# One substitution per group of heads, and both directions' B and Q from one operation, in a hybrid RWKV-7 and attention layer

## The chip, the cores and the metric

The kernel runs on 1 core of a Trainium2 chip. The metric is the device time of one execution in microseconds (us). Before the change it was 1323.57 us, the median of 3 runs (1322.31 to 1329.43).

## What is computed

One layer over 256 latent tokens that read 256 context tokens, width 2048, all in fp32. After a modulated norm, one wide projection feeds two branches: a bidirectional RWKV-7 recurrence with 16 heads of 64, and a latent attention with 8 heads. Both are gated, merged and projected out. The change concerns the recurrence. For each head and direction:

```python
def rwkv7_step(S, xs):
    r, w, k, v, kk, akk = xs
    sa = jnp.einsum("dbhij,dbhj->dbhi", S, -kk)
    S = S * w[..., None, :] + sa[..., :, None] * akk[..., None, :] + v[..., :, None] * k[..., None, :]
    return S, jnp.einsum("dbhij,dbhj->dbhi", S, r)
```

Here kk is the key made a unit vector per head, akk is a * kk with a = sigmoid(...), w is the decay, and k is k * (1 + (a - 1) * k_a). The scan runs over the context and from its last state over the latent tokens, forwards and backwards.

## The kernel before

**Stages.** The modulation and the first projections come first (to about 150 us), then the RWKV stage, to about 900 us, then the attention, then the merge and the output. Projections that nobody waits for soon ("background", tile acc on PE) are strung between the small matmuls of the heads. Each 256 KB piece of weights (tile w, four buffers) is loaded by SP and split into a high and a low part, wh by ACT and wl by DVE; every product is three matmuls (helper mm3).

**The chunked recurrence.** A pair p of heads is one tile of 128 partitions, 64 for each. In the code h counts pairs twice: an even h is the context half of pair h // 2, an odd one its latent half. A half has 4 chunks of 64 tokens in 2 directions, so 8 units, each for two heads. In each unit the step is a lower (or upper) triangular system of 64x64. `front` builds it. It makes th (tanh for a), the sums of the log decay and their exponentials Ep and En, the modified keys km, Q from kk and Ep (in Qbd for a context half, in QR for a latent one), and B and K beside each other in BK. Matmuls of BK with Q give the system, and DVE masks it into AQ.

**The inverse.** `diagonal` inverts the 16x16 blocks on the diagonal of these systems. Eight DMAs write a half's 64 blocks from AQ to DRAM (dl); one DMA reads them back with one block a partition (ln); two copies turn the second direction's blocks round; 14 pairs of DVE operations (pr, then wt) substitute; ACT makes a turned copy; one DMA writes both to DRAM (dw); and eight DMAs put them into WT, the block-diagonal inverse (WTs[0] for context halves, WTs[1] for latent ones). The chain is called a lane. Before, each half has its own lane, appended to `lanes` inside `front`, and the lanes run one after the other. A lane ends only when the levels of the group before are done, since they read WT.

**Groups.** `back` takes a group: halves 2k-1 and 2k, the latent half of one pair and the context half of the next; the first and the last group hold one half, the seven others two. It first builds the whole inverse from WT in levels (matmuls into lv, results in W2 and Z), then goes through the four chunks (tile chp). It starts when both halves' lanes are done (`inverted > hs_[-1]`).

**The order.** `drive` lines the generators up: `back_chain`, `front_chain`, the queue of finals and the queue of lanes, with background work where none may go on. Its clock adds a price for each instruction, so another count of DVE instructions gives another order. A scheduler then sorts each engine's instructions by priority (the lane's substitution runs under `tc.high_priority(HS)`) and by its own estimate of readiness. Every engine and SP's queue work strictly in the order that results. The background list holds gate projections (narrow: 256 columns), keys and values (wide: 512 columns) and others; what the heads' stage leaves is run to the query projections before the attention begins.

Of the kernel before, what the change touches and what calls it, by code (L numbers as in the profile page):

```python
# [9 lines left out]
F32 = mybir.dt.float32  # L10
# [6 lines left out]
P = 128  # L17
# [109 lines left out]
def hybrid_block(  # L127
# [442 lines left out]
    with tc.tile_pool(name="rw", bufs=1) as rw:  # L570
# [99 lines left out]
        def front(h, k, mi, rho):  # L670

            p, lat = h // 2, h % 2
            if not lat:
# [1 line left out]
            ck = cks[p]  # L675
            kk, cr = kks[p], crs.get(p)
            t0 = 0 if lat else T
            WT = WTs[lat]
# [59 lines left out]
            ex = [slice(0, 64), slice(1, 65)]  # L738
            kkc = kk[:, ts].rearrange("p (c t) -> p c t", t=CH)
            for d in range(2):  # L740
                if lat:
                    V.scalar_tensor_tensor(Q[:, d, :, 0], kkc, -1.0, Ep3[d][:, :, ex[d]], ALU.mult, ALU.mult)
                else:
                    for g in range(2):
                        hs = hss[g]
                        V.scalar_tensor_tensor(Q[hs, d, :, g], kkc[hs], -1.0, Ep3[d][hs, :, ex[d]], ALU.mult, ALU.mult)
            BK = rw.tile([P, 8, 2, CH], F32, name="BK", bufs=2)
            BK5 = BK.rearrange("p (d c) a t -> p d c a t", d=2)
            for g in range(2):
                hs = hss[g]  # L750
                for d in range(2):
                    V.scalar_tensor_tensor(BK5[hs, d, :, g], v4(th)[hs, d], 0.5, En3[d][hs, :, ex[1 - d]], ALU.mult, ALU.mult)
                V.tensor_tensor(BK5[hs, :, :, 1 - g], v4(km)[hs], ecols(En, 1, 0)[hs], ALU.mult)
            if lat:
                V.tensor_tensor(Q[:, :, :, 1], dirs(cr), ecols(Ep, 1, 0), ALU.mult)
# [89 lines left out]
                yield  # L845
            halves[h] = (Q, AQ, AR, BKT)

        def diagonal(group, AQ, WT):

            dl = dram.tile([8, 8, 16, 16], F32, name="dl", tag="dl")  # L850
            for g in range(2):
                for b in range(4):
                    r0 = 64 * g + 16 * b
                    nc.sync.dma_start(dl[:, 4 * g + b].rearrange("u r c -> r u c"), AQ[r0:r0 + 16, g, :, 16 * b:16 * b + 16])
            yield LT[0]
            ln = rw.tile([64, 16, 16], F32, name="ln", tag="ln")
            nc.sync.dma_start(ln.rearrange("p r c -> p (r c)"), dl.rearrange("u h r c -> (u h) (r c)"))
            yield LT[1]
            with tc.high_priority(HS):
                wt = rw.tile([64, 2, 16, 16], F32, name="wt")  # L860
# [3 lines left out]
                pr = rw.tile([64, 16, 16], F32, name="pr", tag="ln")  # L864
                for k in range(14, 0, -1):

                    m = 15 - k
                    V.tensor_tensor(pr[:, 0:k, 0:m], X[:, 0:k, k:k + 1].to_broadcast([64, k, m]),
                                    X[:, k, k + 1:16].unsqueeze(1).to_broadcast([64, k, m]), ALU.mult)
# [3 lines left out]
            dw = dram.tile([2, 8, 8, 16, 16], F32, name="dw", tag="dw")  # L873
            yield LT[2]
            nc.sync.dma_start(dw.rearrange("w u h r c -> (u h) w (r c)"), wt.rearrange("p w r c -> p w (r c)"))
            yield LT[3]
            yield lambda: levels >= group
            WTu = WT.rearrange("p w u t -> p (w u) t")
            for g in range(2):
                for b in range(4):  # L880
                    r0 = 64 * g + 16 * b
                    nc.sync.dma_start(WTu[r0:r0 + 16, :, 16 * b:16 * b + 16],
                                      dw[:, :, 4 * g + b].rearrange("w u r c -> r (w u) c"))
            yield LT[4]
            nonlocal inverted
            inverted += 1
# [209 lines left out]
        def front_chain():  # L1096
            nonlocal keyed, fronts
            for k, hs_ in enumerate(groups):
                rho = rw.tile([P, 2, 10], F32, name="rho", bufs=3)
                for m, h in enumerate(hs_):  # L1100
                    p = h // 2
                    yield (lambda: p in cks and (h % 2 == 0 or p in crs))
                    yield from front(h, k, m, rho)
# [466 lines left out]
```

## Time and profile before

| what | value |
|---|---|
| runs | 1323.57 us median, 1322.31 to 1329.43 |
| profiled execution | 1325.01 us, its span 1323.2 us |
| mean granted clock | 0.988 |
| PE, DVE, ACT busy | 95%, 72%, 43% of the span |
| chain that ended last | PE 63%, DMA 17%, DVE 13%, ACT 3% |
| DMA | 212.10 MB, 160 GB/s on average |

PE is TensorE's matmuls, PEld its weight loads, DVE is VectorE, ACT is ScalarE, POOL is GpSimd, SP the queue that issues the DMAs. L103 and L122 are lines of helpers that all matmuls and all elementwise operations pass, so instructions are told apart by their tiles: "wt<-wt,pr" writes wt from wt and pr. A line of groups gives the count, then the busy time and the mean duration in ns, then the engine's idle time before and what ended it. PE's ends are modelled and overlap, so its rate is read from the starts of successive matmuls.

### The profile page before, as it was taken

Reading aid. Unit: us, or ns where it says so; the run is one execution under the profiler, and the core shown is the slowest. Engines: PE = TensorE matmul, PEld = TensorE weight load, DVE = VectorE, ACT = ScalarE, POOL = GpSimd, SP = SyncE. Lnnn points to the kernel's source line nnn. Section 1 sums busy time; section 2 is a strip of 40 time slices with the busy share of each in tenths; the row PEclk is TensorE's granted clock in tenths of the full one; section 3 lists DMA queues with packets and bytes.
Section 4 is the critical chain, followed back from the end, with each engine's and each line's share of the span. In section 5 each row is a group of like instructions: output and inputs, shape, how many; then the busy total and the mean of one; then the engine's idle time right before and its main releaser. Section 6 shows DMA issues by size and latency. Waiting matters only on the chain.

```text
span 1323.2 us, 30169 instructions
## 1 busy us (share of the span) xinstructions
PE 1255.7 (95%) x11484; PEld 1048.0 (79%) x11484; DVE 948.6 (72%) x2658; ACT 570.9 (43%) x1183; POOL 3.3 (0%) x9
## 2 busy tenths in 40 slices
PE   5999888999999999999999999999899999999998
PEld 2656777888887877787788798779788889899776
DVE  4444866878888888878888788655787775468655
ACT  3344532453433524534344245244566645345443
POOL 0000000000000000000000000000000000000000
PEclk9999987999999999999999999999999999999999
DMA  9998554453444423534344244225643326778665
GB/s 375 346 352 298 160 156 120 145 156 90 110 108 127 141 73 95 150 92 124 93 126 141 59 130 130 69 67 174 203 139 104 102 81 217 234 247 272 215 218 175
DMA packets 172320, 212.10 MB, mean 160 GB/s; under 512 B 68560, under 2 KB 96848, under 8 KB 171664
## 3 DMA queue, kind: packets, MB, share of 16 engines
q1 hardware_dynamic: 172176, 210.18, 51.7%
q8 instruction: 90, 1.47, 0.5%
q14 instruction: 54, 0.44, 0.1%
HBM read 195.30 MB, written 14.82 MB: 159 GB/s over the span
## 4 chain that ended last, share of the span: by engine, by line
PE 63%; DMA 17%; DVE 13%; ACT 3%; issue 2%; SPq 1%; DVEq 0%; ACTq 0%
PE acc L103 28%; PE chp L103 11%; PE lv L103 8%; PE wk L103 6%; DMA w<-in_w_proj 5%; DVE wl L122 4%; DMA wm<-in_w_mod_ss 4%; PE a L103 3%; PE ch L103 2%; DMA w<-in_w_out 2%; DVE BK L122 2%; PE wk L107 2%; ACT wh L122 2%; DMA th<-thd 1%; DMA xT<-in_xcT 1%
## 5 line engine op out<-in xcount | busy, mean ns | idle before, releaser
L122 ACT CAST wh<-w 128x512 fp32r<-128x512 f32 (+1 forms) x484 | 290.8, 607 | 387.6 <-PE acc L103 168.2
L122 DVE TENSOR_TENSOR wl<-w,wh 128x512 fp32r<-128x512 f32 (+1 forms) x480 | 322.3, 675 | 150.7 <-ACT wh L122 62.9
L103 PE MATMUL acc<-hmh,wh 128*128 128x256 f32 (+1 forms) x1328 | 423.6, 319 | 6.1 <-ACT wh L122 3.7
L103 PE MATMUL acc<-hml,wh 128*128 128x256 f32 (+2 forms) x1328 | 407.9, 307 | 0.0
L103 PE MATMUL acc<-hmh,wl 128*128 128x256 f32 (+1 forms) x1312 | 401.4, 306 | 3.7 <-DVE wl L122 3.3
L103 PEld LDWEIGHTS acc<-hmh,wh 128*128 128x128 f32 x1328 | 252.3, 190 | 33.2 <-ACT wh L122 7.8
L103 PEld LDWEIGHTS acc<-hmh,wl 128*128 128x128 f32 x1312 | 248.9, 190 | 20.8 <-DVE wl L122 7.9
L103 PEld LDWEIGHTS acc<-hml,wh 128*128 128x128 f32 (+1 forms) x1328 | 251.7, 190 | 10.9 <-issue 1.0
L122 DVE TENSOR_TENSOR pr<-wt 64x14 f32<-64x14 f32 (+6 forms) x224 | 42.5, 190 | 2.5
L122 DVE TENSOR_TENSOR wt<-wt,pr 64x14 f32<-64x14 f32 (+6 forms) x224 | 42.3, 189 | 2.4
L122 DVE TENSOR_TENSOR W<-WT,lv 128x512 f32<-128x512 f32 x48 | 32.7, 684 | 14.4 <-PE lv L103 9.4
L103 PE MATMUL a<-hmh,wh 128*128 128x512 f32 x96 | 41.2, 429 | 0.0
L103 PE MATMUL pm<-wm,ssil 128*32 128x256 f32 x512 | 34.7, 386 | 5.0 <-DMA wm<-in_w_mod_ss 4.9
L103 PE MATMUL a<-hmh,wl 128*128 128x512 f32 x96 | 38.7, 403 | 0.4 <-DVE wl L122 0.4
L103 PE MATMUL lv<-W,Z 64*64 64x64 f32 x1024 | 36.8, 226 | 2.3 <-issue 1.3
L103 PEld LDWEIGHTS lv<-W,Z 64*64 64x64 f32 x1024 | 33.6, 140 | 6.4 <-DVE W L122 1.9
L103 PE MATMUL a<-hml,wh 128*128 128x512 f32 x96 | 38.4, 400 | 0.0
L103 PE MATMUL chp<-obh,wl 128*128 128x256 f32 x128 | 36.5, 285 | 0.3 <-DVE wl L122 0.3
L103 PE MATMUL chp<-obh,wh 128*128 128x256 f32 x128 | 36.2, 283 | 0.0
L103 PE MATMUL chp<-obl,wh 128*128 128x256 f32 x128 | 36.2, 283 | 0.0
L122 DVE TENSOR_TENSOR AQ<-wk,cc 128x256 f32<-128x256 f32 (+1 forms) x48 | 24.4, 509 | 14.4 <-PE wk L103 12.8
L122 ACT ACTIVATE hx<-hx,mod 128x256 f32<-128x256 f32 x32 | 17.5, 594 | 37.8 <-DVE mod L122 37.8
(314 smaller groups left out, 2120.1 us busy)
## 6 DMA issues: line engine op xcount, KB each, us to landing
w<-in_w_proj SPq DMA_DIRECT2D x296, 256.0 KB, 3.0
wm<-in_w_mod_ss SPq DMA_DIRECT2D x64, 512.0 KB, 7.5
w<-in_w_mod_g SPq DMA_DIRECT2D x64, 256.0 KB, 3.4
w<-in_w_br SPq DMA_DIRECT2D x64, 256.0 KB, 3.5
w<-in_w_out SPq DMA_DIRECT2D x64, 256.0 KB, 3.3
w<-in_w_first SPq DMA_DIRECT2D x32, 192.0 KB, 5.2
thd<-th SPq DMA_DIRECT2D x48, 128.0 KB, 2.7
xT<-in_xcT SPq DMA_DIRECT2D x4, 1024.0 KB, 8.9
```

Source lines behind the costliest of these rows:

```text
L103: return self.engine.matmul(out, lhsT=lhsT, rhs=rhs, **kw)
L107: return self.engine.transpose(*a)
L122: return fn(out, *a, **kw)
```

## The change

The lane is made once for a group. `front` only sends its half's blocks out (`blocks_out`), into one of two places of a dl that the group shares. When both halves of the group are through `front`, `diagonal` is appended; it reads up to 128 blocks to 128 partitions, makes four copies, one substitution and one turned copy, writes dw in one DMA for each half, and fills both WT with eight DMAs each. `back_chain` waits for the group's one lane (`inverted > k`).

In `front` the minus sign of Q goes into rnb, the spread inverse norm, so kk is negated from there on. ACT turns th into -0.5 * th - 0.5 in place, and with the negated kk the product is what B held before with its factor 0.5. Q and B are then plain products for both directions in one operation: one for a latent half's Q in place of two, two for a context half's Q in place of four, and two for B in place of four.

```diff
-            V.tensor_copy(rnb.rearrange("p (a c) -> p a c", c=CH), rn.unsqueeze(2).to_broadcast([P, 8, CH]))
+            V.tensor_scalar(rnb.rearrange("p (a c) -> p a c", c=CH), rn.unsqueeze(2).to_broadcast([P, 8, CH]), -1.0, None, ALU.mult)
...
-            V.scalar_tensor_tensor(v4(th), v4(th), 1.0, dirs(kk[:, ts]), ALU.add, ALU.mult)
+            S.activation(th, th, AF.Copy, scale=-0.5, bias=-0.5)
+            V.tensor_tensor(v4(th), v4(th), dirs(kk[:, ts]), ALU.mult)
...
-            for d in range(2):
-                if lat:
-                    V.scalar_tensor_tensor(Q[:, d, :, 0], kkc, -1.0, Ep3[d][:, :, ex[d]], ALU.mult, ALU.mult)
-                else:
-                    for g in range(2):
-                        hs = hss[g]
-                        V.scalar_tensor_tensor(Q[hs, d, :, g], kkc[hs], -1.0, Ep3[d][hs, :, ex[d]], ALU.mult, ALU.mult)
+            kkd = dirs(kk[:, ts])
+            if lat:
+                V.tensor_tensor(Q[:, :, :, 0], kkd, ecols(Ep, 0, 1), ALU.mult)
+            else:
+                for g in range(2):
+                    hs = hss[g]
+                    V.tensor_tensor(Q[hs, :, :, g], kkd[hs], ecols(Ep, 0, 1)[hs], ALU.mult)
...
-                for d in range(2):
-                    V.scalar_tensor_tensor(BK5[hs, d, :, g], v4(th)[hs, d], 0.5, En3[d][hs, :, ex[1 - d]], ALU.mult, ALU.mult)
+                V.tensor_tensor(BK5[hs, :, :, g], v4(th)[hs], ecols(En, 1, 0)[hs], ALU.mult)
...
-            lanes.append(diagonal(k, AQ, WT))
+            blocks_out(AQ, dl[mi])
...
+        def diagonal(group, n, dl, at):
+
+            np_ = 64 * n
             yield LT[0]
-            ln = rw.tile([64, 16, 16], F32, name="ln", tag="ln")
-            nc.sync.dma_start(ln.rearrange("p r c -> p (r c)"), dl.rearrange("u h r c -> (u h) (r c)"))
+            ln = rw.tile([P, 16, 16], F32, name="ln", tag="ln")[0:np_]
+            nc.sync.dma_start(ln.rearrange("p r c -> p (r c)"), dl[0:n].rearrange("m u h r c -> (m u h) (r c)"))
...
-                V.tensor_copy(X[0:32], ln[0:32])
-                V.tensor_copy(X[32:64], ln[32:64].rearrange("p r c -> p c r"))
+                for q in range(2 * n):
+                    qs = slice(32 * q, 32 * q + 32)
+                    V.tensor_copy(X[qs], ln[qs].rearrange("p r c -> p c r") if q % 2 else ln[qs])
...
-            nc.sync.dma_start(dw.rearrange("w u h r c -> (u h) w (r c)"), wt.rearrange("p w r c -> p w (r c)"))
+            for m in range(n):
+                nc.sync.dma_start(dw[m].rearrange("w u h r c -> (u h) w (r c)"),
+                                  wt[64 * m:64 * m + 64].rearrange("p w r c -> p w (r c)"))
...
+            for m in range(n):
+                WTu = WTs[at[m]].rearrange("p w u t -> p (w u) t")
+                for g in range(2):
+                    for b in range(4):
+                        r0 = 64 * g + 16 * b
+                        nc.sync.dma_start(WTu[r0:r0 + 16, :, 16 * b:16 * b + 16],
+                                          dw[m, :, :, 4 * g + b].rearrange("w u r c -> r (w u) c"))
...
+                lanes.append(diagonal(k, len(hs_), dl, [h % 2 for h in hs_]))
...
-                yield (lambda: k in ready and inverted > hs_[-1] and sums_ >= k - 1)
+                yield (lambda: k in ready and inverted > k and sums_ >= k - 1)
```

The order moves with it. Three places in a middle group follow, each before and after. First SP, from the read of the blocks (ln) to the first blocks of the next latent half; WT_1360 is the latent halves' inverse, WT_1358 the context halves'. Before, for the context half alone:

```order
L857 DMA ln<-dl 64x256
L214 DMA w<-in_w_mod_g 128x512
L214 DMA w<-in_w_proj 128x512 x4
L451 DMA thd<-th 128x256
L214 DMA w<-in_w_proj 128x512 x4
L1053 DMA orwd<-y 128x256
L214 DMA w<-in_w_mod_g 128x512 x2
L682 DMA th<-in_wup 128x256
L875 DMA dw<-wt 64x2x256
L882 DMA WT_1358<-dw 16x16x16 x8
L214 DMA w<-in_w_proj 128x512 x3
L854 DMA dl<-AQ 16x8x16 x8
```

And now, for both halves:

```order
L857 DMA ln<-dl 128x256
L214 DMA w<-in_w_mod_g 128x512 x2
L214 DMA w<-in_w_proj 128x512 x2
L1057 DMA orwd<-y 128x256
L877 DMA dw<-wt 64x2x256 x2
L214 DMA w<-in_w_proj 128x512 x2
L886 DMA WT_1360<-dw 16x16x16 x8
L886 DMA WT_1358<-dw 16x16x16 x8
L850 DMA dl<-AQ 16x8x16 x8
```

The latent half's dw and WT moved from ahead of this place into it, and eleven loads of w between ln and dw became four.

Second PE, from the last projection ahead of the context half's first level to the levels of W. Before:

```order
L103 MATMUL acc<-hmh,wh 128x512
L103 MATMUL wk<-QR,BK 128x128 x3
L103 MATMUL lv<-WT_1358,AQ 64x64 x15
L103 MATMUL wk<-QR,BK 128x128 x4
L103 MATMUL lv<-WT_1358,Z 64x64 x16
L103 MATMUL wk<-QR,BK 128x128
L103 MATMUL lv<-W_5635,Z 64x64 x32
L103 MATMUL acc<-hml,wh 128x512
L103 MATMUL acc<-hmh,wl 128x512
L103 MATMUL wk<-QR,BK 128x128 x8
```

And now:

```order
L103 MATMUL acc<-hmh,wl 128x256
L103 MATMUL wk<-cc,sq 128x2 x4
L103 MATMUL lv<-WT_1358,AQ 64x64 x15
L103 MATMUL chp<-UV,AQ 64x64
L103 MATMUL lv<-WT_1358,Z 64x64 x16
L103 MATMUL lv<-W_5360,Z 64x64 x64
L103 MATMUL chp<-UV,AQ 64x64 x3
L103 MATMUL acc<-hmh,wh 128x256
```

The next latent half's QR matmuls went ahead of the levels, and the four rounds of W stand in one run.

Third ACT, at the start of a latent half's `front`, where th and En come from the two low-rank products in wk. Before:

```order
L122 ACTIVATE th<-acc 128x256
L122 COPY wt<-wt 64x256
L122 ACTIVATE th<-wk,dv 128x256 x2
L122 ACTIVATE En<-wk,dv 128x4x64 x2
L122 ACTIVATE En<-En 128x2x4x64
L122 CAST wah<-th 128x256
L122 CAST wh<-w 128x512
L122 COPY AQ<-QR 64x512
L122 ACTIVATE En<-Ep 128x260 x2
L122 ACTIVATE Ep<-Ep 128x260 x2
```

And now:

```order
L122 ACTIVATE th<-wk,dv 128x256 x2
L122 ACTIVATE En<-wk,dv 128x4x64 x2
L122 ACTIVATE th<-th 128x512
L122 CAST wh<-w 128x512
L122 COPY wt<-wt 128x256
L122 ACTIVATE En<-En 128x2x4x64
L122 ACTIVATE cv<-acc,vv 128x512
L122 ACTIVATE En<-Ep 128x260 x2
L122 ACTIVATE Ep<-Ep 128x260 x2
```

The new step th<-th stands between the tanh and the exponentials, and the turned copy of wt, now of 128 partitions, moved behind the tanh.

More of the change, by code (lines that the diff above doesn't have):

```diff
@@ L668, in unit_keys, with front @@
             kks[p] = kk
-        def front(h, k, mi, rho):
+        def front(h, k, mi, rho, dl):
             p, lat = h // 2, h % 2
@@ L677, in front @@
             t0 = 0 if lat else T
-            WT = WTs[lat]
             ts = slice(t0, t0 + T)
@@ L737, in front @@
             Q = rw.tile([P, 2, 4, 2, CH], F32, name="QR", bufs=2) if lat else Qbd
-            ex = [slice(0, 64), slice(1, 65)]
-            kkc = kk[:, ts].rearrange("p (c t) -> p c t", t=CH)
-            for d in range(2):
-                if lat:
-                    V.scalar_tensor_tensor(Q[:, d, :, 0], kkc, -1.0, Ep3[d][:, :, ex[d]], ALU.mult, ALU.mult)
-                else:
-                    for g in range(2):
-                        hs = hss[g]
-                        V.scalar_tensor_tensor(Q[hs, d, :, g], kkc[hs], -1.0, Ep3[d][hs, :, ex[d]], ALU.mult, ALU.mult)
+            kkd = dirs(kk[:, ts])
[5 more added lines that the diff above has]
+                    V.tensor_tensor(Q[hs, :, :, g], kkd[hs], ecols(Ep, 0, 1)[hs], ALU.mult)
             BK = rw.tile([P, 8, 2, CH], F32, name="BK", bufs=2)
@@ L846, in front2, with blocks_out @@
             halves[h] = (Q, AQ, AR, BKT)
-        def diagonal(group, AQ, WT):
-            dl = dram.tile([8, 8, 16, 16], F32, name="dl", tag="dl")
+        def blocks_out(AQ, dl):
             for g in range(2):
@@ L872, in diagonal @@
                 S.copy(wt[:, 1], X.rearrange("p r c -> p c r"))
-            dw = dram.tile([2, 8, 8, 16, 16], F32, name="dw", tag="dw")
+            dw = dram.tile([2, 2, 8, 8, 16, 16], F32, name="dw", tag="dw")
             yield LT[2]
-            nc.sync.dma_start(dw.rearrange("w u h r c -> (u h) w (r c)"), wt.rearrange("p w r c -> p w (r c)"))
+            for m in range(n):
+                nc.sync.dma_start(dw[m].rearrange("w u h r c -> (u h) w (r c)"),
+                                  wt[64 * m:64 * m + 64].rearrange("p w r c -> p w (r c)"))
             yield LT[3]
             yield lambda: levels >= group
[L878 to L883, printed above, removed]
+            for m in range(n):
[5 more added lines that the diff above has]
+                                          dw[m, :, :, 4 * g + b].rearrange("w u r c -> r (w u) c"))
             yield LT[4]
@@ L1099, in front_chain @@
                 rho = rw.tile([P, 2, 10], F32, name="rho", bufs=3)
+                dl = dram.tile([2, 8, 8, 16, 16], F32, name="dl", tag="dl")
                 for m, h in enumerate(hs_):
@@ L1102, in front_chain @@
                     yield (lambda: p in cks and (h % 2 == 0 or p in crs))
-                    yield from front(h, k, m, rho)
+                    yield from front(h, k, m, rho, dl)
                     keyed += 1
+                lanes.append(diagonal(k, len(hs_), dl, [h % 2 for h in hs_]))
                 yield lambda: backs >= k
```

8 lines of the change are left out of this document (4 added, 4 removed).

## The prediction

> **What bounds the kernel now.** I read the page first, then the sums by stage, the waits of the middle stage, the groups by shape, and the timeline of one group of heads. The page gives the span and the engines:
>
> ```profile
> span 1323.2 us, 30169 instructions
> PE 1255.7 (95%) x11484; PEld 1048.0 (79%) x11484; DVE 948.6 (72%) x2658; ACT 570.9 (43%) x1183; POOL 3.3 (0%) x9
> ```
>
> The profiled execution took 1325.0 us by its own clock, 1.8 over its span and 1.4 over the median of 1323.6. I make the sum against 1325.0 and take 1.4 off at the end. The change touches only the RWKV part, so its stages matter. The columns are the stretch, its length, busy time of PE, PEld, DVE, ACT and POOL, the granted clock, the DMA share and GB/s:
>
> ```profile
> 200.00:245.00 45.00, 40.86 (x399) 35.41 (x397) 31.05 (x104) 13.85 (x28) 0.00 (x0) 0.85 0.49 144
> ...
> 476.00:564.00 88.00, 84.14 (x941) 69.87 (x940) 71.88 (x222) 35.15 (x75) 0.00 (x0) 1.00 0.41 112
> 564.00:651.00 87.00, 84.75 (x949) 70.29 (x945) 72.67 (x223) 35.13 (x75) 0.00 (x0) 1.00 0.41 113
> ...
> 1108.00:1131.00 23.00, 23.00 (x198) 23.00 (x198) 12.24 (x19) 11.43 (x22) 0.00 (x0) 1.00 0.75 225
> ```
>
> Two middle groups of heads take 88 and 87 us each. PE is idle for 3.9 and 2.3 us of them, DVE for 16.1 and 14.3 us, ACT for more than half. So PE sets the pace of a group, and its small gaps are all that faster work elsewhere can return. The gaps that have a releaser on DVE, between 250 and 880 us (what waited, then the total, the number of waits and the longest):
>
> ```profile
> ACT wh L122 <- PE acc L103: 113.1, 55, 13.4
> ...
> PEld wk L103 <- DVE BK L122: 5.3, 5, 1.2
> PEld wk L103 <- DVE QR L122: 4.7, 4, 1.2
> ...
> PEld chp L107 <- DVE rvb L122: 4.2, 6, 0.9
> ```
>
> PE waits for DVE 14.2 us in the three largest rows (5.3 + 4.7 + 4.2); in most others the engine that waits is ACT or DVE, and it waits for PE. That is how a stage reads whose bound is PE.
>
> **The change, part by part.** The durations (busy total, mean ns of one) by shape:
>
> ```profile
> L122 DVE TENSOR_TENSOR pr<-wt 64x14 f32<-64x14 f32 (+6 forms) x224 | 42.5, 190 | 2.5
> L122 DVE TENSOR_TENSOR wt<-wt,pr 64x14 f32<-64x14 f32 (+6 forms) x224 | 42.3, 189 | 2.4
> ```
>
> ```profile
> L122 DVE SCALAR_TENSOR_TENSOR BK<-th,En 64x256 f32<-64x256 f32 x64 | 24.6, 416 | 0.5
> L122 DVE TENSOR_TENSOR BK<-km,En 64x512 f32<-64x512 f32 x32 | 21.8, 682 | 0.1
> L122 DVE SCALAR_TENSOR_TENSOR Qbd<-kk,Ep 64x256 f32<-64x256 f32 x32 | 13.3, 417 | 0.4
> L122 DVE TENSOR_TENSOR km<-km,ck 128x512 f32<-128x512 f32 x16 | 11.0, 687 | 0.2
> L122 DVE SCALAR_TENSOR_TENSOR th<-th,kk 128x512 f32<-128x512 f32 x16 | 10.8, 674 | 0.0
> ...
> L122 DVE SCALAR_TENSOR_TENSOR QR<-kk,Ep 128x256 f32<-128x256 f32 x16 | 6.0, 410 | 0.0
> L122 DVE TENSOR_TENSOR QR<-cr,Ep 128x512 f32<-128x512 f32 x8 | 5.5, 690 | 0.1
> ```
>
> ```profile
> L122 ACT COPY wt<-wt 64x256 f32<-64x256 f32 x16 | 10.2, 638 | 4.8 <-DVE wt L122 4.5
> L122 ACT ACTIVATE En<-En 128x512 f32<-128x512 f32 x16 | 10.1, 634 | 0.4
> ```
>
> 1. *One substitution a group.* There are 16 now, one a head, and 9 afterwards, one a group (seven groups of two heads, two of one). The elements a partition stay the same and only the partitions double; the 64x256 operation at 417 ns and the 128x256 one at 410 show that partitions cost nothing. So 7/16 of 42.5 + 42.3 = 84.8 us go: 37.1 us of DVE. The copies out of ln stay 32. ACT's turned copy goes from 16 to 9: 7 x 0.638 = 4.5 us less.
> 2. *B and Q of both directions from one operation.* B: 64 operations of 24.6 us become 32 like the km row, 21.8: 2.8 less. Q of context heads: 13.3 us become 16 x 0.682 = 10.9: 2.4 less. Q of latent heads: 6.0 become 8 x 0.690 = 5.5: 0.5 less. The product with kk is a plain one, 11.0 for 10.8: 0.2 more. The sign put into rnb turns a copy into an operation with a constant:
>
> ```profile
> L122 DVE TENSOR_SCALAR km<-th,dv 128x512 f32<-128x512 f32 x16 | 8.7, 541 | 5.3 <-ACT th L122 5.3
> ...
> L122 DVE COPY rnb<-rn 128x512 f32<-128x512 f32 x8 | 3.3, 415 | 0.1
> ```
>
> At most that is 8 x (0.541 - 0.415) = 1.0 us more, at least nothing; the km row has two constants, this one has one, and I take nothing.
>
> 3. *A new step on ACT.* The factor -0.5 and the shift of th become an ACT operation like the En row: 16 x 0.634 = 10.1 us. ACT as a whole: 10.1 - 4.5 = 5.6 more, at 43% busy.
>
> DVE is thus 37.1 + 2.8 + 2.4 + 0.5 - 0.2 = 42.6 us lighter. Almost all of that lies beside PE's work, which covers it. What reaches the end is the part of 14.2 us that PE waits for DVE. A group's DVE time falls from 72 to about 66 us; I let half of the waits go: 7 us, with 0 and 14 as ends.
>
> *The ACT step on the path.* B now waits for DVE, ACT and DVE again. In ACT's order the step stands between the tanh and the exponentials of the same head, which B and Q wait for anyway; so a head's B comes at most 0.63 us later. PE waited at B or Q nine times: 9 x 0.63 = 5.7 us at most, 0 at least, and I take 3, the middle, as some waits vanish with the lighter DVE. By the Trainium skill ("TensorE: Matmul & The Clock Gate", the section on the array of 32x32 blocks) ACT's queue is strictly first in, first out, so the step would stand behind any ACT instruction that waits: at the mean wait of the wh row, 113.1/55 = 2.1 us, nine times make 19 us in place of 3. The trace agrees that ACT holds its place (13.4 us at one wh); I keep 3 because nothing new stands ahead of the step.
>
> *PE's order.* The matmuls are the same in number. What differs is how often PE goes from one kind to another. Counted in the two orders, neighbours that write different tiles are 922 before and 865 after, 57 fewer, most of them between projections (acc) and the small matmuls of the heads. What one costs:
>
> ```profile
> 487.50 0.28 PE L103 MATMUL acc<-hml,wh 128*128 128x256 f32 x1
> ...
> 487.61 0.28 PE L103 MATMUL acc<-hmh,wl 128*128 128x256 f32 x1
> 487.82 0.19 PEld L103 LDWEIGHTS chp<-AR,UV 128*64 128x64 f32 x2
> 487.82 0.33 PE L103 MATMUL chp<-AR,UV 128*64 128x64 f32 x2
> ...
> 488.08 0.39 PE L103 MATMUL acc<-hmh,wh 128*128 128x256 f32 x1
> ```
>
> Projections follow each other at 0.11 us. The detour takes 487.61 to 488.08, 0.47; less 0.11 it is 0.36 for two switches and two small passes, so at most 0.18 a switch; the way out alone is 0.21 - 0.11 = 0.10. With 0.10 to 0.18, 57 are 6 to 10 us. I take 0.12, near the lower end since the passes are in the upper one: 7 us less.
>
> *Projections moved behind.* The order of a middle group holds 48 narrow projections fewer than before (144 or so for 192), and the last group begins with 42 narrow and 104 wide ones more left over. They run after the heads, where PE is dense (23.00 of 23.00 us in a stretch of such work); each costs there what it cost before. Zero, as long as weights arrive; the DMA share of 0.75 there is the cover.
>
> *One lane a group.* The blocks of a group now go out, through the substitution and back as one chain, which starts when the second head is ready. The chain of the second head before, on SP, DVE and PE:
>
> ```profile
> 523.56 3.65 SPq L854 DMA_DIRECT2D dl<-AQ  x8
> ...
> 549.02 0.63 SPq L875 DMA_DIRECT2D dw<-wt  x1
> 551.77 3.77 SPq L882 DMA_DIRECT2D WT<-dw  x8
> ```
>
> ```profile
> 534.77 0.67 DVE L122 COPY wt<-ln 32x256 f32<-32x256 f32 x2
> ...
> 548.10 0.17 DVE L122 TENSOR_TENSOR wt<-wt,pr 64x14 f32<-64x14 f32 x1
> ```
>
> ```profile
> 521.64 1.16 PE L103 MATMUL wk<-Qbd,BK 128*128 128x128 f32 x8
> ```
>
> ```profile
> 549.84 0.40 PE L103 MATMUL acc<-hml,wh 128*128 128x512 f32 x1
> 550.08 0.39 PE L103 MATMUL acc<-hmh,wl 128*128 128x512 f32 x1
> 550.40 1.15 PE L103 MATMUL lv<-WT,AQ 64*64 64x64 f32 x32
> ...
> 556.53 0.27 PE L103 MATMUL lv<-WT,AQ 64*64 64x64 f32 x1
> ```
>
> ```profile
> WT<-dw SPq DMA_DIRECT2D x128, 16.0 KB, 2.1
> ```
>
> Before, the latent head's inverse was long in place (its lane ran ahead) and only the context head's was late. Now dw is two DMAs and WT sixteen in a row. From the last Qbd matmul at 521.6: WT would begin at 551.77 + 0.63 = 552.4; the latent eight are issued by 556.2 and landed 2.1 us later, 36.7 us after that matmul; the context eight 3.8 us later, at 40.4. What covers it on PE: the first level matmul came 28.8 us after, with 27 wide and 96 narrow projections between; now there are 78 and 48. At 0.24 (550.08 less 549.84) and 0.11 that is 17.0 before and 24.0 after, 7 us more: 35.8 for the latent head, and some 41 for the context one, which came 6.1 us behind it and comes nearly as far behind now. Need and cover agree within a microsecond, so I put 0 here, with a loss as the open end. Behind WT on SP stand eight dl DMAs of the next latent head (3.65 us), and behind those the weights that ACT's wh waits for; PE has the levels to do meanwhile, which need none.
>
> Sum: -7 (waits for DVE) + 3 (ACT step) - 7 (switches) + 0 + 0 = -11: 1325.0 - 11 = 1314.0, on the scale of the median 1312.6 us.
>
> **The rivals.**
>
> *A: the lane comes late (slower).* It is one mechanism: PE, in order, stands at the first level matmul of a group until the sixteen WT DMAs have landed. The price is seven groups times the lateness. For it: the cover above has no margin, and between ln and dw SP has few weight loads, so a substitution later than planned also holds up weights that queue behind dw. Against it: DVE is lighter, and the substitution took 13.3 us (534.77 to 548.10) for some 5.3 us of its own work, so it can shorten. It decides from about 2.5 us a group: 7 x 2.5 = 17.5 brings 1312.6 to 1330. At 4 us a group, the time of the eight added WT DMAs, it is 28 us: 1341. The trace shows what idling adds: 0.85 of the clock in 200 to 245, where PE idled 4.1 of 45 us. The Trainium skill (same page, the part on the HAM clock gate) has the clock halved after an idle window of about 3.4 us and given back after a busy one; an estimate by that page is 1.7 us more for each stall of 4 us, 12 in all, and 1353. Here only the 0.85 bears on it.
>
> *B: DVE sets the pace after all (much faster).* DVE works in order at 72 of 88 us. If each of PE's starts hung on it, the whole 42.6 us would show: 1281, and with half of it 1302. Against it: PE's 2.3 to 3.9 idle us a group.
>
> *C: nothing that can be measured.* The waits stay, at other places, and the switches were covered: 1325.0 - 0 to 5, so 1318 to 1324 on the median's scale.
>
> **How the numbers follow.** My forecast has 0.48. Its own ends are 1300 (14 and 10 less, no cost of the step) and 1323 (6 less, 5.7 more), with most of the chance between 1303 and 1319. A has 0.18 (1330 to 1345), B 0.12 (1281 to 1302), C 0.22. About 0.5% (6.6 us, so 1317 to 1330) is what a measurement can tell from no change here. Faster by more: 0.43 of the forecast and all of B, 0.55. Within: 0.05 of the forecast and C, 0.27. Slower: A, 0.18. The range leaves a tenth on each side: the faster part of B below 1296, the slower half of A above 1337.
>
> **What would show it.** Right: DVE busy near 906 us and ACT near 576, 126 each of pr and wt at 190 ns, PE idle in a middle group no more than 3 us, its cycle about 80 us, and the long dense stretch after the heads some 30 us longer. The switch term: PE's busy time falls by 5 us or more. Wrong: PE rows that wait for WT<-dw or, behind it, for w, at the first lv of a group (A); PE's idle time in the groups unchanged and the span with it (C); a group's cycle at 75 us or less with the same stretch behind it (B).

## The result, and the profile after

The changed kernel takes 1338.88 us (median of 4 runs, 1337.81 to 1341.97), the kernel before 1322.94 (4 runs, 1317.63 to 1329.43). The ratio is 1.0123, 95% interval 1.0089 to 1.0156: slower by 1.2%. The prediction said 1312.6 and had its chance of 0.55 on faster; it had the wrong sign, and the time lies above its range, which ended at 1337.

The first lines of the page of the changed kernel, whose profiled execution took 1337.81 us:

```profile
span 1336.0 us, 29950 instructions
PE 1253.1 (94%) x11484; PEld 1050.9 (79%) x11484; DVE 926.1 (69%) x2399; ACT 577.5 (43%) x1192; POOL 3.3 (0%) x9
```

PE is busy 2.6 us less than before and the span is 12.8 us longer: PE stands idle 15.4 us more. To see where, here are the sums by stage. The first row of each kernel runs from the end of the first group's levels to the end of the last group's; the second goes on to the start of the attention. The kernel before:

```profile
227.00:878.00 651.00, 634.42 (x6990) 528.90 (x6989) 528.86 (x1609) 261.25 (x566) 0.00 (x0) 1.00 0.40 112
878.00:930.00 52.00, 50.56 (x485) 45.70 (x482) 30.85 (x90) 22.52 (x52) 0.00 (x0) 1.00 0.50 150
```

The changed kernel:

```profile
230.00:860.00 630.00, 595.22 (x6789) 503.15 (x6788) 496.08 (x1336) 255.84 (x549) 0.00 (x0) 0.98 0.39 108
860.00:948.00 88.00, 85.54 (x660) 73.58 (x655) 42.06 (x112) 33.35 (x75) 0.00 (x0) 0.98 0.45 137
```

The heads end earlier, because projections were moved behind them, and the stretch behind grows by more: 651 + 52 = 703 us before, 630 + 88 = 718 after. Of these 15 us, PE's idle time among the heads is 18.2 (651 - 634.4 = 16.6 before, 630 - 595.2 = 34.8 after) and that behind them 1.0; PE's busy time in both falls by only 4.2. The last column but two is TensorE's granted clock, as a share of full speed: 1.00 before, 0.98 after. Rows around the places where it falls, in the changed kernel:

```profile
545.00:552.00 7.00, 5.52 (x111) 4.87 (x112) 4.60 (x13) 1.35 (x3) 0.00 (x0) 0.76 0.57 176
702.00:715.00 13.00, 11.11 (x134) 9.83 (x134) 7.61 (x21) 1.72 (x3) 0.00 (x0) 0.61 0.29 87
736.00:743.00 7.00, 6.73 (x86) 5.63 (x86) 2.43 (x7) 2.79 (x8) 0.00 (x0) 0.76 0.08 27
794.00:804.00 10.00, 4.82 (x26) 4.60 (x27) 4.72 (x9) 4.50 (x10) 0.00 (x0) 0.66 0.47 130
```

If the clock is half there and full outside, the half-clock times are 7 x 0.24 x 2 = 3.4 us, then 10.1, 3.4 and 6.8: 23.7 us among the heads, which cost at most half of it, 11.9. They are inside PE's busy time, so without them that time would have fallen by 4 to 16 us, not by 4.2.

Waits between 250 and 880 us in the kernel before (what waited, for what, then the total, the number of waits and the longest):

```profile
PE wk L103 <- DVE QR L122: 3.0, 4, 0.8
...
PE acc L103 <- ACT wh L122: 0.5, 2, 0.2
```

and in the changed kernel:

```profile
PE wk L103 <- DVE QR L122: 7.6, 5, 3.3
...
PE acc L103 <- ACT wh L122: 6.8, 2, 6.2
```

The waits of PE at QR have become longer each (up to 3.3 us, 0.8 before), and PE waits 6.2 us for one split weight (wh).

The longest wait at QR in the timeline, whose columns are the start, the duration, the engine and what ran (in brackets the wait ahead of it and what ended it), on SP first:

```profile
695.10 7.80 SPq L886 DMA_DIRECT2D WT<-dw  x16
703.00 0.39 SPq L214 DMA_DIRECT2D w<-in_w_mod_g  x1
```

and then on PE, where the next row of projections comes only at 715:

```profile
700.28 0.33 PE L103 MATMUL lv<-WT,AQ 64*64 64x64 f32 x2
703.89 1.19 PE L103 MATMUL wk<-QR,BK 64*128 64x128 f32 x6 [3.29 <-DVE QR L122]
705.01 1.96 PE L103 MATMUL lv<-WT,AQ 64*64 64x64 f32 x30
```

For 7.8 us SP issues WT and no weights. From 700.3 us on PE has the levels, the next head's QR and no projection. It stands 3.3 us at QR, and the 30 level matmuls that follow take 1.96 us; 32 took 1.15 before, at the full clock.

Of the 6.8 us at wh, 6.2 are one wait, at 799, and it does not stand behind WT. SP ahead of it:

```profile
783.85 0.43 SPq L1419 DMA_DIRECT2D gd<-gT  x1
784.95 3.96 SPq L214 DMA_DIRECT2D w<-in_w_proj  x3
789.95 1.24 SPq L877 DMA_DIRECT2D dw<-wt  x2
...
801.58 7.70 SPq L886 DMA_DIRECT2D WT<-dw  x16
```

and the DMAs issued from 783 to 797 us, with KB each and the median time from issue to landing:

```profile
w<-in_w_proj SPq DMA_DIRECT2D x5, 256.0 KB, 12.0
dw<-wt SPq DMA_DIRECT2D x2, 128.0 KB, 11.4
```

Each kernel issues gd once: 8 KB that it writes to DRAM one element of 4 bytes at a time (of the 2532 DMA packets in that stretch 2115 are under 512 B). What SP issues around and behind it here lands after 11 to 12 us, where from 200 to 783 us the medians are 3.0 for w and 2.4 for dw. ACT's split of such a weight, PE behind it and SP's own WT wait for these. In the kernel before SP issues nothing in the 7 us behind its gd. The 25 us from gd's issue, first before, then after:

```profile
735.00:760.00 25.00, 23.45 (x356) 20.11 (x352) 17.22 (x53) 4.57 (x10) 0.00 (x0) 1.00 0.23 49
783.90:808.90 25.00, 18.48 (x161) 17.11 (x162) 16.75 (x44) 10.56 (x23) 0.00 (x0) 0.86 0.41 79
```

PE's idle time there is 1.6 us before and 6.5 after, and the clock costs at most 25 x 0.14 = 3.5 us more. So by an estimate from these rows up to 8 us of the loss lie where the new order has put other DMAs behind gd. No run moved gd, so this is read from the traces and not shown by an experiment.

### The profile page after: what moved, and what is told of

The parts are those of the page before. It is cut to its first block, busy times and chain, and to the rows that moved or that the text cites. A ratio compares the mean times of both kernels' runs of the same rounds, so it can differ in the third digit from the quotient of the medians.

```text
span 1336.0 us, 29950 instructions
## 1 busy us (share of the span) xinstructions
PE 1253.1 (94%) x11484; PEld 1050.9 (79%) x11484; DVE 926.1 (69%) x2399; ACT 577.5 (43%) x1192; POOL 3.3 (0%) x9
## 4 chain that ended last, share of the span: by engine, by line
PE 37%; DMA 9%; DVE 7%; ACT 2%; issue 1%; SPq 1%; DVEq 0%; ACTq 0%
PE acc L103 16%; PE chp L103 8%; PE lv L103 6%; PE wk L103 3%; PE ch L103 3%; DVE wl L122 2%; DMA w<-in_w_proj 2%; DMA th<-thd 1%; DMA w<-in_w_out 1%; PE wk L107 1%; DMA thd<-th 1%; DMA dw<-wt 1%; ACT wh L122 1%; DVE wt L122 1%; DMA ln<-dl 1%
## 5 line engine op out<-in xcount | busy, mean ns | idle before, releaser
L122 ACT CAST wh<-w 128x512 fp32r<-128x512 f32 (+2 forms) x484 | 291.2, 607 | 378.6 <-PE acc L103 134.4
L103 PE MATMUL acc<-hml,wh 128*128 128x256 f32 (+1 forms) x1328 | 405.3, 305 | 0.0
L103 PEld LDWEIGHTS acc<-hmh,wl 128*128 128x128 f32 x1312 | 248.8, 190 | 23.7 <-DVE wl L122 10.6
L103 PEld LDWEIGHTS acc<-hml,wh 128*128 128x128 f32 x1328 | 251.4, 189 | 11.1 <-issue 0.9
L103 PE MATMUL pm<-wm,ssil 128*32 128x256 f32 x512 | 34.8, 385 | 5.6 <-DMA wm<-in_w_mod_ss 5.4
L103 PE MATMUL wk<-QR,BK 64*128 64x128 f32 x256 | 25.3, 308 | 10.7 <-DVE QR L122 7.6
L103 PE MATMUL chp<-UV,AQ 128*64 128x64 f32 x512 | 30.2, 235 | 3.7 <-ACT AQ L122 2.4
L103 PEld LDWEIGHTS pm<-wm,ssil 128*32 128x32 f32 x512 | 13.3, 109 | 24.6 <-DMA wm<-in_w_mod_ss 13.3
```

The source lines that it names most:

```text
L103: return self.engine.matmul(out, lhsT=lhsT, rhs=rhs, **kw)
L122: return fn(out, *a, **kw)
```

## The experiments

Each run is given as the ratio to the kernel before on the same chip. Four theories stood at the start. Theory 1, lost cover: the planner's clock is charged less for DVE, so a group holds fewer projections, and PE stands among the small matmuls. Theory 2, the merged lane. Theory 3, the ACT step and the merged B and Q make QR late. Theory 4: any other order moves the time by a per cent.

**One half of the change at a time.** The first run has only the B and Q half:

```diff
-            V.scalar_tensor_tensor(v4(th), v4(th), 1.0, dirs(kk[:, ts]), ALU.add, ALU.mult)
+            S.activation(th, th, AF.Copy, scale=-0.5, bias=-0.5)
+            V.tensor_tensor(v4(th), v4(th), dirs(kk[:, ts]), ALU.mult)
...
-                for d in range(2):
-                    V.scalar_tensor_tensor(BK5[hs, d, :, g], v4(th)[hs, d], 0.5, En3[d][hs, :, ex[1 - d]], ALU.mult, ALU.mult)
+                V.tensor_tensor(BK5[hs, :, :, g], v4(th)[hs], ecols(En, 1, 0)[hs], ALU.mult)
```

with Q and the sign in rnb likewise.

> The kernel before with the B and Q half of the change alone (sign in rnb, ACT step on th, merged Q and B); the lanes are as before, one a half. In its order the middle groups still hold 208 narrow and 96 to 99 wide projections, and 1392 narrow ones stand behind the heads, as before. Theory 1 (the loss is cover: the order puts fewer projections among the small matmuls of a group, and PE stands there for DVE and ACT): no change from before, 1316 to 1328. Theory 2 (the merged lane: its longer chain on SP and DVE is late, or holds up the weights behind it): no change or a few us less, 1312 to 1326. Theory 3 (the ACT step and the merged operations make B and Q late): the loss is here, 1333 to 1342. Theory 4 (any other order moves the time by about 1% either way): anything from 1310 to 1340.

Measured: 1314.55 us for 1316.53, ratio 0.9978 (0.9958 to 0.9998). The waits of PE at BK and QR between 250 and 880 us did not grow:

```profile
PEld wk L103 <- DVE QR L122: 3.3, 3, 1.3
PEld wk L103 <- DVE BK L122: 3.3, 4, 1.0
```

They are 4.7 and 5.3 us before, and PE's idle time among the heads is 13.2 us for 16.6. Theory 3 falls: this half is no loss, if anything a small gain.

The second run has only the lane:

```diff
-            lanes.append(diagonal(k, AQ, WT))
+            blocks_out(AQ, dl[mi])
...
+                lanes.append(diagonal(k, len(hs_), dl, [h % 2 for h in hs_]))
```

> The kernel after with the B and Q half taken back: only the merged lane is new. The order is close to that of after: the middle groups hold 124 to 221 narrow projections, and 1488 stand behind the heads (1434 in after, 1392 before). Theory 1 (lost cover): slow like after or a little worse, 1333 to 1345. Theory 2 (the lane itself): the same, 1333 to 1345. Theory 3 (ACT step, late B and Q): back at the level of before, 1316 to 1328.

Measured: 1357.87 us, ratio 1.0303 (1.0276 to 1.0331). The loss is in the lane and the plan that comes with it, and larger than in the whole change.

**Cover, and a control for the plan.** LF is the part of a chain's planned latency that the planner waits before its next step.

```diff
-LF = 0.6
+LF = 0.75
```

> The kernel after with one number of the planner changed: LF 0.75 for 0.6, so that each step of a chain waits a larger part of the planned latency and more projections are put between. All instructions are those of after, in another order: the middle groups hold 193 to 208 narrow and 96 wide projections, 1392 stand behind the heads, as before. Theory 1 (lost cover): the loss goes, 1305 to 1325, and PE's idle time among the heads falls from 46 us to the 23 us of before. Theory 2 (the lane itself): the loss stays, 1332 to 1345, with PE or the split of the weights waiting behind dw and WT. Theory 3: stays too, 1332 to 1345, with waits for QR and BK.

Measured: 1342.79 us, ratio 1.0204 (1.0171 to 1.0237). The groups are as full as before and the loss is not smaller. Theory 1 in this form falls. PE's idle time among the heads is 25.0 us in place of 34.8.

The same number at 0.62 in the kernel before:

> The kernel before with the planner's LF at 0.62 for 0.6: the same instructions in a slightly other order (1362 narrow projections behind the heads, 789 changes of tile for 785). It shows how far a harmless change of the plan moves the time. Theories 1 to 3: within 5 us of before, 1317 to 1328. Theory 4 (any other order moves it by 1%): 1310 or less, or 1335 or more.

Measured: 1322.40 us, ratio 1.0045 (1.0026 to 1.0063). This one harmless change of the plan moves the time by half a per cent. Its profile says where: dw stands behind gd there, PE waits 6.4 us for WT, and the clock over the 25 us from gd's issue is 0.80. A larger change of the same number (LF 0.75, further below) gives 0.9930. So plans of the kernel before span 1.15%; 2 or 3% are more than that, but the 1.2% of the whole change alone could not be told from theory 4.

**What about the lane.** Two forms: SP (its dw and its sixteen WT stand ahead of the weights), or the longer chain itself. The lane's DMAs go to GpSimd's queue:

```diff
-                        nc.sync.dma_start(WTu[r0:r0 + 16, :, 16 * b:16 * b + 16],
+                        nc.gpsimd.dma_start(WTu[r0:r0 + 16, :, 16 * b:16 * b + 16],
```

and dl, ln and dw likewise, first in the changed kernel, then with LF 0.75, then in the kernel before as a control.

> The kernel after with the lane's DMAs (dl, ln, dw, WT) issued by GpSimd's queue instead of SP's; the operations are the same. It tells apart two forms of theory 2, since theories 1 and 3 fell with the first four runs. Theory 2a (SP stands for the merged substitution at dw and then issues sixteen WT in a row; the weights behind them are late, ACT stands at their split in its queue, and the exponentials behind that, QR and PE follow): the waits of PE at QR of 1.4 to 3.5 us in a group go, and the time falls to 1305 to 1322. Theory 2b (the one longer chain from the second half's blocks to WT is late by itself, whatever queue issues it; the plan has put the next latent half's QR beside the levels): 1330 to 1345, with the same waits. If GpSimd's queue is slow by itself, PE would wait at the first lv for WT, which the run below with the lanes of before would show as well.

Measured: 1334.07 us, ratio 1.0119 (1.0097 to 1.0140), which is no better than the change itself.

> The same move of the lane's DMAs to GpSimd's queue in the kernel with LF 0.75, whose groups hold as many projections as before (208 narrow and 96 wide). Theory 2a: the 2.4-us waits at QR and the half-clock windows after them go; 1305 to 1322, against 1343 with SP's queue. Theory 2b: 1335 to 1348.

Measured: 1319.39 us, ratio 1.0012 (0.9989 to 1.0034), against 1.0204 on SP. PE's idle time among the heads falls to 18.5 us and the granted clock there is 1.00.

> The control: the kernel before with its lanes' DMAs on GpSimd's queue. Theory 2a: SP stood there for dw and issued WT as well, but only eight in a row and with PE covered; 0 to 8 us less than before, 1308 to 1318. Theory 2b: no change, 1313 to 1322. A slow queue: over 1325, with PE waiting at lv for WT.

Measured: 1326.29 us, ratio 1.0054 (1.0035 to 1.0072). GpSimd's queue is no gift by itself: PE waited up to 3.1 us at lv for its WT.

The first two runs disagree, and their orders say how they differ. In the first the plan shifted with the queue: counted in the traces among the heads, neighbours on PE that write different tiles rose from 510 to 589, and at the prediction's 0.12 us each 79 of them eat 9 us (PE's busy time in the whole execution rose from 1253.1 to 1262.4). It also keeps a cost at gd, with 5.2 us of PE's idle time in 25 and a clock of 0.86, where the second has 2.1 and 1.00. In the second the changes of tile are 545 against 550. So the pair with LF 0.75 is the one in which little but the queue differs, and there the queue is worth 1.9%. The next two runs part it further, in that plan.

Only WT on GpSimd's queue:

> The kernel after with LF 0.75, and only the sixteen WT DMAs of a lane on GpSimd's queue; dw stays on SP, which still stands for the substitution there. The other half of the question is the next run. Theory 2a-burst (the weights are late because sixteen WT, 7.8 us, go ahead of them on SP): near 1320, the time with the whole lane moved (1319 against 1343 with nothing moved). Theory 2a-stand (SP stands at dw for the end of the substitution): stays at 1335 to 1343. Both alike: about 1331.

Measured: 1322.53 us, ratio 1.0030 (1.0012 to 1.0049).

Only dw there (the same edit in the line that writes dw):

> The kernel after with LF 0.75, and only the dw DMAs on GpSimd's queue, so SP no longer stands for the substitution; the sixteen WT stay on SP. SP must then still wait at WT until dw has landed. Theory 2a-stand: near 1320. Theory 2a-burst: stays at 1335 to 1343. Both alike: about 1331.

Measured: 1343.75 us, ratio 1.0201 (1.0173 to 1.0230). Only WT matters: moving it brings back 1.7 of the 2.0%, moving dw nothing. SP's standing at dw is innocent; the sixteen WT in a row are not. One group with LF 0.75 and WT on SP, on SP, ACT and PE:

```profile
546.93 0.42 SPq L214 DMA_DIRECT2D w<-in_w_proj  x1
547.88 8.61 SPq L886 DMA_DIRECT2D WT<-dw  x16
556.59 0.87 SPq L214 DMA_DIRECT2D w<-in_w_mod_g  x2
```

```profile
551.13 0.62 ACT L122 CAST wh<-w 128x512 fp32r<-128x512 f32 x1 [2.82 <-DMA w<-in_w_proj]
```

```profile
553.90 0.33 PE L103 MATMUL lv<-WT,AQ 64*64 64x64 f32 x2
556.48 0.98 PE L103 MATMUL wk<-QR,BK 64*128 64x128 f32 x10 [2.26 <-DVE QR L122]
557.38 1.97 PE L103 MATMUL lv<-WT,AQ 64*64 64x64 f32 x30
```

The same group with WT on GpSimd's queue, on SP and PE:

```profile
547.07 5.53 SPq L214 DMA_DIRECT2D w<-in_w_proj  x4
```

```profile
550.48 0.30 PE L103 MATMUL lv<-WT,AQ 64*64 64x64 f32 x2 [0.34 <-DMA WT<-dw]
551.13 0.64 PE L103 MATMUL acc<-w,ssil 128*32 128x256 f32 x8
...
554.51 1.14 PE L103 MATMUL lv<-WT,AQ 64*64 64x64 f32 x30
555.58 1.16 PE L103 MATMUL wk<-QR,BK 64*128 64x128 f32 x16
```

SP goes on with weights, the order puts projections between the first two level matmuls and the other 30, and QR is ready when PE comes to it. The link between WT and the wait is this order. With WT on SP, no instruction in these rows waits for a weight issued behind WT: the one for which ACT waits 2.82 us was issued at 546.93, ahead of it, and DVE works without a pause up to QR. PE only comes to QR with too little put in between. The order is made when the kernel is built, by the scheduler's own estimate of when weights are there; how much of the loss a late weight would make at run time was not tried apart from it. The whole run of levels of that group (first lv to last lv), on SP:

```profile
553.90:578.70 24.80, 22.35 (x334) 19.03 (x334) 15.26 (x35) 4.62 (x8) 0.00 (x0) 0.79 0.38 105
```

on GpSimd's queue:

```profile
550.40:567.60 17.20, 16.90 (x328) 14.72 (x329) 14.49 (x34) 5.15 (x9) 4.44 (x9) 1.00 0.50 120
```

Nearly as many matmuls take 24.8 us and 17.2. Of the 7.6 us, the clock is at most 24.8 x 0.21 = 5.2 and PE's idle time 2.45 - 0.30 = 2.2. For comparison, such a run in the kernel before, with eight WT on SP ahead of it, and one in the changed kernel:

```profile
550.40:571.20 20.80, 19.98 (x324) 16.59 (x323) 18.47 (x43) 5.84 (x13) 0.00 (x0) 1.00 0.23 55
```

```profile
535.50:553.90 18.40, 15.79 (x318) 14.12 (x317) 13.43 (x41) 3.17 (x6) 0.00 (x0) 0.91 0.34 90
```

PE's idle time in it is 0.8 us before and 2.6 after.

The other way round, the burst alone put into the kernel before:

```diff
-            for g in range(2):
+            for g in [0, 1, 0, 1]:
                 for b in range(4):
```

> The kernel before with the eight WT DMAs of every lane issued twice (the second time the same data to the same place), so that sixteen stand on SP in a row as in after; 128 DMAs and 3.8 us of SP a lane more, nothing merged. The order shifts with it: the levels of a group are spread over its projections (80 to 153 narrow ones between). Theory 2a-burst: slower, by 8 us or more (over 1326), with waits for the weights and for QR behind WT. Theory 2a-stand, or a fault of the merged chain alone: within 5 us of before, 1313 to 1325.

Measured: 1385.17 us, ratio 1.0504 (1.0478 to 1.0530); among the heads PE is idle 44.3 us of 720 and the clock is 0.96. The sign fits, but this run tells little: its plan splits the levels into pieces, and PE's waits are at AQ (9.4 us) and Z (6.1) inside them and for the split weights (6.2 at wh, 5.9 at wl), none of them at QR behind the burst.

**Half of WT moved.** Eight of the sixteen go to GpSimd's queue, so that eight stand in a row on SP as before:

```diff
-                        nc.sync.dma_start(WTu[r0:r0 + 16, :, 16 * b:16 * b + 16],
+                        (nc.gpsimd if m else nc.sync).dma_start(WTu[r0:r0 + 16, :, 16 * b:16 * b + 16],
```

> The kernel after as it is (LF 0.6), with one thing moved: of a lane's sixteen WT DMAs the eight of the second half of the group go to GpSimd's queue, so that eight stand on SP in a row as before the change. The plan stays that of after (734 changes of tile for 728, 150 to 164 narrow projections in the middle groups). Burst alone is the cause: the loss of 1.2% goes, 1308 to 1324, and the half-clock windows among the heads with it. The lost cover has a part of its own: between, 1325 to 1334. Burst has no part in after's own plan: 1334 to 1342.

Measured: 1331.11 us, ratio 1.0075 (1.0049 to 1.0102). In the change's own plan 0.5 of the 1.2% go, though the two intervals overlap; PE's idle time among the heads falls from 34.8 to 26.5 us. The expectation had this as "the lost cover has a part of its own". The trace shows another part, the one at gd: in the 25 us from its issue PE is idle 6.8 us and the clock is 0.86, as in the changed kernel, so moving WT has left that cost whole.

> The same split of WT between the two queues in the kernel with LF 0.75. The burst on SP is back to eight, and GpSimd's queue has eight in place of sixteen, so PE should wait less at lv than with all sixteen there (1322.5 against 1317.4 of before). Burst: 1306 to 1318, as good as the kernel with the B and Q half alone or better. If eight on SP already do harm in the merged lane: 1325 to 1335.

Measured: 1323.25 us, ratio 1.0024 (1.0006 to 1.0042), so 1.8 of 2.0% go. It is not as good as expected. Three of its groups still wait 2.1 us at QR:

```profile
548.56 0.44 PE L103 MATMUL lv<-WT,AQ 64*64 64x64 f32 x4
551.09 0.90 PE L103 MATMUL wk<-QR,BK 64*128 64x128 f32 x10 [2.09 <-DVE QR L122]
551.92 2.07 PE L103 MATMUL lv<-WT,AQ 64*64 64x64 f32 x60
```

but behind this wait 60 level matmuls take 2.07 us, at the full clock; on SP 30 took 1.97.

**LF 0.75 without the lane.**

First the kernel before with LF = 0.75:

> The kernel before with LF 0.75: the planner's number of the runs above without the merged lane. Its plan stretches the heads over more of the projections (1080 narrow ones left behind, 1392 before). If LF 0.75 is a gain by itself, the runs with the merged lane, LF 0.75 and WT moved (1.0012 to 1.003 of before) hide a loss of the lane: then 1300 to 1311. If it is neutral or a cost here, the lane without its burst is worth about nothing: 1313 to 1335. The burst theory says nothing else of this run than that half-clock windows among the heads stay rare (two at most), since eight WT stand in a row.

Measured: 1311.85 us, ratio 0.9930 (0.9904 to 0.9955).

Then the kernel with the B and Q half alone and LF = 0.75:

> The B and Q half alone with LF 0.75; its plan is like the run before this one. It is the other candidate for a kernel that beats both (the B and Q half alone with LF 0.6 was 0.9978 of before). The B and Q half should be worth as much here as there: 2 to 4 us less than the run before this one, whatever that is.

Measured: 1306.13 us, ratio 0.9897 (0.9876 to 0.9918): this kernel beats both by more than the interval. Its heads:

```profile
231.00:907.00 676.00, 666.95 (x7338) 566.90 (x7337) 546.57 (x1595) 289.68 (x623) 0.00 (x0) 0.99 0.42 119
```

PE is idle 9.0 us of 676. With half of WT moved and the same LF, but the merged lane:

```profile
230.00:876.00 646.00, 624.18 (x6962) 521.95 (x6958) 505.43 (x1357) 264.44 (x569) 31.26 (x56) 0.99 0.41 111
```

21.8 of 646. DVE has 546.6 - 505.4 = 41 us less to do there in a stage that is 30 us shorter, and PE idles 12.8 us more. So LF 0.75 is a gain by itself in the kernel before (0.9930) and hid a loss: the kernel with the merged lane, without its burst, still takes 1.0024/0.9897 of the one with B and Q alone, 1.3% more. The two plans differ as well, with 6962 matmuls of PE among the heads against 7338, so this is the price of the lane together with its plan.

## Why the prediction was wrong

*What bounds the kernel.* Right: PE sets the pace. PE's idle time among the heads and the clock go with the ratios in the main: 9.0 us for 0.9897, 13.2 for 0.9978, 16.6 before, 34.8 for 1.0123, 34.9 with a clock of 0.97 for 1.0303. The idle time alone does not rank them: LF 0.75 with WT on SP has 25.0 us and 1.0204.

*DVE lighter by 42.6 us.* The durations were right. The changed kernel's groups:

```profile
L122 DVE TENSOR_TENSOR wt<-wt,pr 128x14 f32<-128x14 f32 (+13 forms) x126 | 24.6, 195 | 1.8
L122 DVE TENSOR_TENSOR pr<-wt 128x14 f32<-128x14 f32 (+13 forms) x126 | 24.6, 195 | 1.7
...
L122 DVE TENSOR_TENSOR BK<-th,En 64x512 f32<-64x512 f32 x32 | 21.9, 684 | 0.4
```

84.8 us became 49.2, 35.6 less where 37.1 were forecast, and B 24.6 became 21.9. All durations of DVE's records add up to 1067.7 us before and 1025.3 after, 42.4 less. But DVE's busy time, which counts a moment once, fell by 22.5 us only. Records overlap, the short ones above all. In the kernel before:

```profile
536.25 0.14 DVE L122 TENSOR_SCALAR rs_y<-rs_z 128x4 int32<-128x4 int32 x1
...
536.34 0.18 DVE L122 TENSOR_TENSOR wt<-wt,pr 64x14 f32<-64x14 f32 x1
```

A sum of mean durations counts the overlap twice; it made the relief nearly twice as large as it was.

*ACT 5.6 more.* Nearly right (570.9 to 577.5, 6.6 more), and its step on the path, 3, was nothing: the run with this half alone was no slower.

*Waits for DVE, -7.* This term failed in the change: PE's idle time among the heads grew by 18.2 us in place of -7. The B and Q half alone did return 3.4 us of it (16.6 to 13.2), and 7.9 with LF 0.75 (16.9 to 9.0), so the lane's share of DVE's relief is the one that brought nothing.

*Switches, -7.* In line with the trace: PE's busy time fell by 4.2 us although up to 11.9 of half clock are in it. No run tried the term alone.

*One lane a group, 0.* This is the step that failed first: the term stood at 0, and the lane alone took 41.3 us more than before (1357.87 for 1316.53). The prediction counted need and cover up to the first level matmul and found them even. That was right: PE hardly waited for WT. Of the queue behind WT it said that "PE has the levels to do meanwhile, which need none". There lay the error that the runs show. The levels are a chain of small matmuls that waits for DVE and ACT at each step, and what fills PE between them is projections, which need weights. With sixteen WT in a row SP sends none for 7.8 us, the order holds fewer projections there, and PE stands. Runs of nearly one plan (550 and 538 changes of tile among the heads) show that WT's place is the cause there: 1.0204 with it on SP, 1.0030 with it elsewhere. In the change's own plan half of WT moved gave 0.5%, with intervals that overlap. There the count also left out which DMAs the new order would put behind gd, up to 8 us by the estimate from the trace.

*Rival A* had the right culprit, the sixteen WT, and the right side, but another place: PE was to stand at the first lv until WT had landed. It stands one step later, at QR. Its second price was right: the clock. The prediction's estimate by the Trainium skill ("TensorE: Matmul & The Clock Gate", the part on the HAM clock gate) was 12 us for that; 23.7 us at half clock cost at most 11.9. That the two agree is luck: the estimate has seven stalls of 4 us, the trace four stretches, the longest behind a wait of 3.3 us and one of 6.8 us at gd.

*Projections moved behind, zero.* True for their own cost, as far as the sums show. Whether they count as cover is not shown: with all lane DMAs off SP, the fuller plan has 1.0012 and the thinner one 1.0119, but that thinner plan also has more changes of tile and the cost at gd.

*What stays open.* In the plan of the change, half of WT moved brings 0.5%; the rest, 0.75% (some 10 us), is not parted between the cost at gd, which by the trace can be most of it, thinner cover and the lane's longer chain. A run with gd issued elsewhere would part them. Nor is the lane's 1.3% in the last comparison: waits at QR with half of WT moved, waits for WT at lv with all of it, are what the profiles show. Why the lane alone loses 3.0% and the whole change 1.2% was not tried; its trace has 572 changes of tile among the heads for 510, and one wait of 8.0 us behind gd.

## What to carry to other kernels

Merging two small chains makes one burst on the queue that issues them; before counting what the merged arithmetic saves, count what else goes through that queue, and for how long it gets nothing. On the engine that sets the pace, look at the stretch where it runs a dependent chain: there its filler is worth most, and filler needs its loads just then. Relief of an engine that waits is worth at most the waits for it that end a stage. And a new order moves every DMA: look what now stands behind one that is slow by itself, however small it is.

## What the hardware showed beside

The half clock came without a long stop. With LF 0.75 and WT on SP, the longest waits around it are 2.3 us, and it lasted through a stretch in which PE was busy nearly all the time:

```profile
557.00:567.50 10.50, 10.31 (x124) 9.05 (x123) 5.31 (x14) 0.70 (x2) 0.00 (x0) 0.51 0.33 104
```

That is 10.5 x 0.49 x 2 = 10.3 us of half clock, three times the 3.4 us of the shortest one in the changed kernel. PE's busy share was 98% in it, with 124 small matmuls; a stretch of 10 us at the same place with WT moved holds 245. The Trainium skill ("TensorE: Matmul & The Clock Gate", the part on the HAM clock gate) has the clock halved after an idle window of about 3.4 us and restored after a busy one. The lengths agree with such a window; that a stop must last 3.4 us, or that a busy PE by the profile's count restores the clock, this trace does not show. A wait of 2.1 us with half of WT moved passed with no half clock, so the wait alone does not decide it.

GpSimd's queue issued the sixteen WT in about 9.9 us:

```profile
544.99 2.22 POOL L886 DMA_DIRECT2D WT<-dw  x4 [78.19 <-DVE wl L122]
548.17 6.67 POOL L886 DMA_DIRECT2D WT<-dw  x12 [0.96 <-issue]
```

SP took 7.8 in the changed kernel and 8.6 in the group above with LF 0.75. GpSimd's is a slower queue, but not the one that the weights go through.
